# A float32 gradient matmul on one core: four warm-up matmuls in place of 55, and a new order of visits on every engine

## The chip, the cores and the metric

The kernel runs on one core of one Trainium2 chip. The metric is device time in microseconds (us) of one execution, lower is better; the figure is the median of several runs. A core has five engines with queues of their own: TensorE (PE in the profile; its weight loads are PEld), VectorE (DVE), ScalarE (ACT), GpSimd (POOL) and SyncE (SP), and 16 DMA engines that move data between the chip's memory and the on-chip memory.

## The reference

```python
batch, m, k, n = 16, 512, 1024, 768
# input: batch x m x k, grad_output: batch x m x n, both float32
grad_weight = np.einsum('bmk,bmn->kn', input, grad_output)   # 1024 x 768, float32
```

With batch and m taken together this is one product: X transposed times G, where X has 8192 rows of 1024 and G 8192 rows of 768. The sum runs over the 8192 rows.

## The kernel before

**Units.** The 8192 rows come in 32 units of 256 rows, two groups of 128 (128 is the height of TensorE's array). The loads convert to bf16 on the way and are issued by GpSimd, for each unit first `gp` (rows of G), then `xp` (rows of X), L170 to L182. The first 128 rows of unit 0, and the X rows behind them, come in float32 (`gf`, `xf`) by the queues of SyncE and ScalarE and are cast in pieces on VectorE and ScalarE (`round_by`, L222 to L240; the tokens r0 to r4 below are five of these pieces). Ten buffers hold units (`PAIRS_HELD`).

**Blocks.** The 1024 x 768 result is cut into four blocks: A and B are the upper 512 rows, left and right 384 columns, C and D the lower rows, left and right. Each block has four tiles of 128 x 384, numbered 0 to 3 (`q`). Units 0 to 4 and 31 (kind "s" in `LOADS`) are multiplied plainly: each of their two row groups adds one matmul to each of the 16 tiles. The 26 units between (kind "P") are multiplied with seven products in place of eight, by sums of halves made on VectorE: `sum_x` (three instructions, L206, L208, L210) and `sum_g` (L216, L218, L220) into `xe` and `ge`, and two of them back into the unit's own buffers. The seven products are the streams A, B, C and 1, 5, 6, 7; A and 1 share one accumulation. At the end the streams 1, 5, 6, 7 are combined into A to D by VectorE and GpSimd (`close` with `final`, `merge`).

**Banks and sums.** TensorE adds up in eight banks of its accumulator memory. Stream A stays in banks 0, 1 and 2 all the time, packed (`PLACES`): tiles 1 and 2 are split in a 256- and a 128-column piece, so that a matmul of A1 or A2 is two instructions. All other tiles share the remaining banks: a tile gets a few matmuls, then its sum is moved out and the bank goes to another tile. There are four ways to move sums:

- `close` (L348): the bank is copied or added to the tile's sum in on-chip memory (`acc`, `macc`), on VectorE (token v, an addition, L371) or on ScalarE (token c, a copy, only where nothing has to be added, L367);
- `fill` (f, L302): ScalarE copies the tile's sum into a bank first, so that TensorE goes on adding to it;
- `set_aside` (z, L383): the bank is copied into one of 24 spare tiles, `aside`, and
- `add_aside` (y, L392) adds it to the sum later, on VectorE.

**Order.** All of it is written out by hand: `PLAN` is a list of tokens, and the loop at L401 emits them one after the other; nothing is reordered afterwards. Each engine runs its own instructions in the order of the list. A token such as `C1@6.1` is one matmul of tile C1 into bank 6, opened there; `A2.1` is one more matmul of A2; `vC1`, `cC3` close a tile; `fD1@6` fills bank 6 with D1; `zcC2.0` sets C2 aside by ScalarE into spare tile 0, `yC2.0` adds it; `g0.5` is the first of the three sums of G's part of unit 5, `x2.5` the last of X's; `wC1` is a merge on GpSimd. Finished tiles are stored by SyncE's queue (one piece by ScalarE's), the first of them in two halves.

**Warm-up.** Ahead of the first product TensorE multiplies constants (L156 to L164) while the first data are on their way: one matmul of 512 columns, then 54 of 80 columns with a stationary operand of 32 columns, all bf16, each with a weight load of its own.

```python
WARMUP = [("b", 512)] + [("s", 80)] * 54
```

Of the kernel before, what the change touches and what calls it, by code (L numbers as in the profile page):

```python
# [9 lines left out]
P = 128  # L10
# [1 line left out]
LOADS = "sssssPPPPPPPPPPPPPPPPPPPPPPPPPPs"  # L12

PLAN = (
    "A2.1 C1@6.1 C3@3.1 C2@4.1 vC1 C0@5.1 cC3 A0.1 A1.1 r0 cC2 A3.1 B2@7.1 D0@3.1 r1 r3 D2@6.1 D1@4.1 r2 "
    "r4 vB2 C0.1 cD0 A0.1 vD1 A1.1 B1@7.2 cD2 B3@3.2 vB1 B0@6.2 cB3 D3@4.2 vB0 C3@7.1 C2@3.1 cD3 A2.1 vC3 "
    "A3.2 fD1@6 A1.1 vC2 D0@7.2 fB2@4 D1.2 fD2@3 vD0 B2.2 cD1 C0.1 D2.2 vB2 C1@7.2 cD2 B0@6.2 vC1 B1@4.2 "
    "B3@3.2 vB0 C2@7.2 vB1 fC3@6 A0.2 vB3 A2.2 D3@4.2 vC2 C3.2 vD3 B2@3.1 C1@7.1 cC3 C0.1 vB2 A1.1 D0@4.1 "
    "D1@6.1 vC1 A3.1 D2@3.1 vD0 fB0@7 vD1 C0.2 B1@4.2 vD2 B2@6.2 vB1 B0.2 B3@3.2 vB2 cB0 C2@4.2 vB3 A0.2 "
    "zcC2.0 D2@6.2 fD3@3 C3@7.2 yC2.0 D0@4.2 zcD2.1 vC3 D3.2 D1@6.2 vD0 cD3 C1@7.2 yD2.1 A3.4 fB3@3 vD1 "  # L30
    "A2.4 vC1 D3@4.2 A1.4 zcD3.0 B1@6.2 yD3.0 B3.2 vB1 C2@4.2 cB3 D0@7.2 vC2 D2@6.2 zcD0.1 C3@3.2 vD2 "
    "fD1@4 C0.2 B0@7.2 zvC3.0 C1@6.2 yD0.1 zcB0.2 B2@3.4 vC1 D1.4 yC3.0 vB2 D0@7.2 cD1 C3@6.2 yB0.2 "
    "zcD0.1 A0.2 g0.5 A0.2 fC2@4 D3@7.2 zvC3.0 C2.2 g1.5 zcD3.2 B1@6.2 yD0.1 cC2 D2@3.2 zvB1.3 B3@7.2 "
    "zcD2.1 B0@4.1 g2.5 B0.1 zcB3.4 C1@6.1 x0.5 C1.2 zcB0.5 A2.3 yC3.0 zcC1.6 10@3.1 x1.5 12@7.1 A1.3 c10 "
    "yD3.2 c12 C2@4.1 x2.5 C3@6.1 C0.1 zcC2.0 g0.6 C0.2 zcC3.2 11@3.1 yB1.3 13@7.1 A3.2 c11 g1.6 A3.1 c13 "
    "50@4.1 yD2.1 51@6.1 52@3.1 c50 A0.1 g2.6 53@7.1 x0.6 c51 A0.1 70@4.1 C0.1 c52 A1.1 v53 71@6.2 c70 "
    "72@3.1 x1.6 72.1 c71 73@7.2 yB3.4 c72 60@4.2 x2.6 61@6.2 c73 g0.7 62@3.2 c60 63@7.2 v61 c62 A2.1 "
    "g1.7 B0@4.2 c63 yC1.6 B2@3.2 zcB0.3 B1@6.1 g2.7 B1.1 A3.1 zcB2.1 yB0.5 13@4.2 zcB1.4 11@7.1 x0.7 "
    "11.1 A2.1 zc13.6 A0.1 v11 C0.1 C1@3.2 x1.7 10@6.2 zcC1.5 yC2.0 B3@4.2 zc10.7 53@7.1 g0.8 53.1 A3.1 "
    "A1.1 zc53.0 x2.7 70@3.2 vB3 51@6.2 zc70.8 C2@7.1 g1.8 C2.1 zc51.9 yC3.2 12@4.2 C3@3.1 zcC2.10 g2.8 "  # L40
    "C3.1 A1.1 x0.8 A0.1 zcC3.2 50@7.2 52@6.3 v12 zc50.11 71@3.1 x1.8 71.1 zc52.12 A2.1 yB0.3 72@4.2 "
    "zc71.13 73@7.1 g0.9 73.1 zc72.3 A3.1 x2.8 61@6.2 zc73.14 g1.9 63@3.2 v61 C0.1 60@4.2 zc63.15 g2.9 "
    "B2@7.2 y13.6 zc60.16 B1@6.2 zcB2.17 10@3.1 x0.9 10.1 A3.1 f62@4 C0.1 vB1 A2.1 zc10.6 50@7.2 x1.9 "
    "62.2 zc50.18 yB2.1 C2@3.2 c62 51@6.1 x2.9 51.1 A1.1 fB0@7 g0.10 A0.1 B3@4.3 vC2 B0.2 zcB3.1 g1.10 "
    "B0.1 12@3.2 v51 cB0 11@4.1 g2.10 11.1 zc12.19 13@6.3 yB1.4 zc11.20 C3@7.1 x0.10 C3.2 C1@3.3 v13 "
    "53@4.1 x1.10 53.2 zcC1.4 70@6.3 vC3 zc53.21 x2.10 52@3.2 zc70.22 g0.11 71@7.2 zc52.23 61@4.2 yC1.5 "
    "A2.1 f62@6 A0.1 g1.11 B2@3.2 v71 62.2 zcB2.5 C0.1 g2.11 A1.1 c62 x0.11 A1.1 A3.2 f73@3 72@7.2 v61 "
    "f60@6 A2.1 73.1 x1.11 73.2 f12@4 v72 60.3 c73 x2.11 12.2 c60 g0.12 63@7.3 c12 y53.0 B1@3.3 f10@6 "
    "g1.12 11@4.2 v63 10.2 zc11.0 g2.12 A0.1 C2@7.3 vB1 c10 C0.1 x0.12 f51@4 C0.1 B0@6.2 f50@3 51.3 vC2 "
    "x1.12 50.3 f52@7 vB0 A0.1 c51 52.1 g0.13 52.1 c50 A1.1 13@4.1 x2.12 13.1 fB3@6 A2.1 g1.13 C1@3.2 c52 "  # L50
    "v13 B3.3 fC3@7 g2.13 A3.1 vC1 53@4.2 cB3 C3.1 x0.13 C3.2 f70@3 C0.1 A0.1 f71@6 v53 70.3 cC3 x1.13 "
    "71.3 c70 y10.7 72@4.2 c71 x2.13 72.1 61@7.1 g0.14 f62@3 61.2 A1.1 v72 fB2@6 A2.1 62.2 g1.14 f10@4 "
    "62.1 v61 B2.3 c62 g2.14 10.2 f11@7 x0.14 10.1 A3.2 cB2 12@3.3 v10 f73@6 x1.14 11.3 v12 73.2 c11 "
    "x2.14 73.1 60@4.1 f63@3 g0.15 60.2 C0.1 c73 y70.8 A0.1 63.2 fB0@7 g1.15 63.1 B1@6.3 v60 c63 B0.1 "
    "g2.15 fC1@4 B0.2 vB1 A1.2 fC2@3 x0.15 A2.2 f13@6 C1.3 vB0 C2.2 cC1 x1.15 C2.1 13.3 y51.9 f50@7 C0.1 "
    "g0.16 cC2 51@4.3 c13 x2.15 50.2 g1.16 f52@3 50.1 v51 53@6.3 c50 g2.16 52.3 fC3@4 v53 A0.2 fB3@7 "
    "x0.16 C3.3 c52 yC2.10 B3.3 f72@6 x1.16 cC3 70@3.3 vB3 72.2 f62@4 g0.17 72.1 f71@7 A3.2 x2.16 62.2 "
    "c72 g1.17 62.1 71.3 v70 fB2@6 C0.1 c62 g2.17 B2.3 v71 f11@4 61@3.1 x0.17 61.2 f12@7 11.3 cB2 v61 "
    "12.2 c11 x1.17 12.1 73@6.3 yC3.2 c12 10@3.1 x2.17 10.2 f60@7 g0.18 63@4.3 v73 60.3 g1.18 fB1@6 A1.2 "
    "v10 A2.2 c60 g2.18 B1.3 v63 A0.2 x0.18 cB1 C0.2 f50@4 C1@3.3 y52.12 A3.1 x1.18 A3.1 50.3 vC1 B0@7.1 "  # L60
    "x2.18 B0.2 c50 g0.19 13@6.3 fC2@3 vB0 A1.1 f53@4 A2.1 C2.1 g1.19 C2.2 v13 53.3 cC2 g2.19 51@7.1 "
    "x0.19 f52@6 51.2 A0.1 c53 A2.1 v51 52.3 f70@3 x1.19 52.1 fC3@4 61@7.3 y50.11 c52 C3.1 g0.20 C3.2 "
    "f72@6 70.1 x2.19 70.2 cC3 g1.20 72.3 v61 c70 C0.1 g2.20 B3@4.4 c72 y71.13 fB2@7 A1.2 y72.3 f71@6 "
    "A3.2 x0.20 B2.3 vB3 12@3.3 cB2 x1.20 71.4 v12 62@7.1 g0.21 62.3 c71 x2.20 f63@3 60@4.2 g1.21 60.1 "
    "f10@6 A0.1 v62 63.3 g2.21 f11@7 10.4 v60 c63 x0.21 11.4 fC1@4 v10 fB1@3 C0.2 c11 A2.1 x1.21 A2.1 "
    "C1.3 y63.15 f73@6 fB0@7 B1.1 x2.21 B1.2 g0.22 cC1 73.4 cB1 y60.16 B0.1 f13@4 g1.22 B0.3 v73 C2@3.2 "
    "cB0 g2.22 C2.1 13.1 x0.22 f51@6 13.3 f53@7 vC2 A1.2 c13 51.1 x1.22 51.3 f50@3 y73.14 53.2 c51 x2.22 "
    "53.2 g0.23 50.4 c53 yB2.17 A0.2 f52@7 g1.23 A3.2 c50 y10.6 70@6.2 g2.23 70.1 f72@3 C3@4.4 y50.18 "
    "x0.23 A2.2 C0.2 v70 72.3 x1.23 f61@6 72.1 52.3 vC3 c72 x2.23 52.1 61.2 g0.24 c52 61.2 y12.19 B3@4.3 "
    "c61 g1.24 B3.1 f12@7 B2@3.4 y11.20 f62@6 g2.24 12.1 x0.24 12.3 62.3 vB2 c12 A1.2 vB3 c62 60@7.2 "  # L70
    "x1.24 f71@3 60.1 A0.1 g0.25 A0.1 fB1@4 A3.2 x2.24 f63@6 71.2 g1.25 71.2 v60 B1.2 c71 g2.25 B1.2 "
    "yB3.1 63.3 f11@3 x0.25 63.1 cB1 C1@7.4 c63 y53.21 11.2 f10@4 x1.25 11.2 f73@6 vC1 10.3 c11 x2.25 "
    "10.1 fC2@7 73.1 g0.26 73.3 c10 yC1.4 C2.2 fB0@3 g1.26 C2.2 c73 y70.22 13@4.3 cC2 g2.26 B0.4 y52.23 "
    "f50@6 x0.26 f53@7 A2.3 cB0 50.4 v13 f51@3 x1.26 53.4 f70@4 v50 51.1 g0.27 51.3 f61@6 x2.26 c53 70.2 "
    "g1.27 70.2 c51 yB2.5 B3@7.2 c70 g2.27 B3.1 61.3 y11.0 f52@3 C0.1 fC3@4 x0.27 C0.3 c61 A1.3 vB3 x1.27 "
    "A0.3 fB2@7 x2.27 C3.2 g0.28 C3.2 52.2 cC3 g1.28 52.2 72@6.1 g2.28 72.3 c52 A3.3 v72 B2.2 x0.28 f62@6 "
    "B2.2 12@4.2 cB2 x1.28 12.2 60@3.1 f71@7 x2.28 60.4 v12 62.1 g0.29 62.4 fB1@4 v60 B1.2 c62 g1.29 B1.2 "
    "f11@3 g2.29 71.4 vB1 63@6.2 c71 x0.29 63.2 11.4 v63 A2.1 x1.29 fC1@6 A2.2 v11 C2@4.3 g0.30 f13@3 "
    "C2.1 10@7.1 x2.29 10.3 vC2 C1.2 g1.30 C1.2 f11@4 v10 13.3 cC1 g2.30 13.1 A1.1 x0.30 A1.2 c13 12@6.2 "
    "f13@3 11.1 x1.30 10@7.1 A0.3 c11 v12 13.1 x2.30 f61@4 C0.3 v10 f62@6 61.4 v13 f60@7 62.2 f63@3 v61 "  # L80
    "60.2 A3.3 v62 f71@4 63.2 v60 f72@6 71.2 v63 f70@7 A0.2 A1.2 v71 f73@3 A2.3 f51@4 wC1 A3.2 73.5 vA3 "
    "vA0 72.3 v73 51.4 vA1 f53@3 wC3 70.4 vA2 53.4 v72 f52@0 v70 fC1@1 C0.2 52.3 v51 fC2@2 f50@6 C1.3 wB1 "
    "fC3@7 vC0 C2.3 fD1@4 v52 C3.5 cC1 wB2 fD2@5 50.4 v53 fB1@1 fD3@0 D2.2 wB3 B1.4 vC2 cC3 fB2@3 v50 "
    "D1.2 cB1 D3.2 B2.5 fD0@2 vD2 fB0@7 vD3 D0.2 fB3@1+6 vB2 B0.7 vD0 vD1 B3.6 vB0 cB3 "
).split()


WARMUP = [("b", 512)] + [("s", 80)] * 54
PAIRS_HELD = 10
SUMS_HELD = 8  # L90
ASIDE = 24

MERGED = 2


PACKED = True
PLACES = {
    0: [(0, 0, 0, 384)],
    1: [(0, 384, 0, 128), (1, 0, 128, 384)],
    2: [(1, 256, 0, 256), (2, 0, 256, 384)],  # L100
    3: [(2, 128, 0, 384)],
}

HALVED = 3


@with_exitstack
def kernel(  # L110
    ctx: ExitStack,
    tc: tile.TileContext,
    input: bass.AP,
    grad_output: bass.AP,
    out: bass.AP,
):
    nc = tc.nc
    bf16 = mybir.dt.bfloat16
    f32 = mybir.dt.float32
# [34 lines left out]

    wps = psum.tile([P, 512], f32, name="bank7")
    for dt, cols in WARMUP:  # L156
        rows = 32 if dt == "s" else P
        nc.tensor.matmul(
            wps[0:rows, 0:cols],
            nc.const_aps.tensor(1.0, (P, rows), bf16),  # L160
            nc.const_aps.tensor(1.0, (P, cols), bf16),
            start=True,
            stop=True,
        )  # L164
# [4 lines left out]
    for u, kind in enumerate(LOADS):  # L169
# [15 lines left out]
        tiles[u] = (xp, gp)  # L185
        if kind == "P":
            items.append(("P", u, None))

    extra = {}
# [77 lines left out]
            return macc[:, SLOT[p], q, :]  # L270
        row = q if p in "AB" else Q + q
        return acc[:, row, LEFT if p in "AC" else RIGHT]

    SHARED = {"A": "1", "B": "6", "C": "7", "D": "5", "6": "1", "7": "6"}
# [180 lines left out]
```

## Time and profile before

| | |
|---|---|
| time, median of 3 runs | 161.84 us (161.83 to 162.16) |
| profiled execution, first to last instruction (span) | 160.0 us |
| the median over that span | 1.84 us |
| PE busy, matmuls | 155.1 us, 1057 |
| DVE busy, instructions | 146.8 us, 344 |
| ACT busy, instructions | 118.2 us, 274 |
| POOL busy | 39.6 us |
| loaded and stored by the core's DMA engines | 33.42 MB, mean 209 GB/s |
| matmul of 384 columns, start to start, full clock | 0.162 us |
| first real matmul, last real matmul (starts) | 5.29 us, 156.43 us |

The profile is of one execution, and its own time is the span of 160.0 us with what lies around the first and last instruction, which the median puts at 1.84 us. The busy time of an instruction is its latency: VectorE and ScalarE begin the next one before the last has ended, so that an addition of 128 x 384 that is listed with 0.55 us follows another after 0.46 us. Matmuls overlap in the same way: 0.326 us listed, 0.162 us from start to start.

| line, engine | what | number, mean |
|---|---|---|
| L328 PE | matmul, 128 x 384 | 838, 0.33 us |
| L371 DVE | add a bank to a sum | 83, 0.56 us |
| L392 DVE | add a spare tile to a sum | 46, 0.56 us |
| L206 to L220 DVE | sums of halves, six for each of 26 units | 156, 0.36 to 0.69 us |
| L302 ACT | fill a bank from a sum | 118, 0.48 us |
| L367 ACT | close a bank by copying | 107, 0.48 us |
| L383 ACT | set a bank aside | 43, 0.48 us |

### The profile page before, as it was taken

The numbers are of one execution on the slowest core, as the hardware profiler recorded it, in microseconds if no ns is written. First come the engines' busy times: TensorE is split into PE (matmuls) and PEld (weight loads), VectorE is DVE, ScalarE is ACT, GpSimd is POOL, SyncE is SP. The second block draws the span as 40 slices with busy tenths as digits, with TensorE's granted clock in tenths as the row PEclk, the third lists the DMA queues.
The fourth block names the chain that finished last, engine by engine and source line by source line (L and its number), as shares of the span: only waits on it lengthen the run. The fifth ranks groups of instructions, "written<-read, shape, count | busy, mean of one in ns | idle before, by whom it ended". The sixth has DMA issues, their size and how long they took to land.

```text
span 160.0 us, 3074 instructions
## 1 busy us (share of the span) xinstructions
PE 155.1 (97%) x1057; PEld 98.4 (62%) x1057; DVE 146.8 (92%) x344; ACT 118.2 (74%) x274; POOL 39.6 (25%) x74
## 2 busy tenths in 40 slices
PE   8999899999999999999999999999999999999991
PEld 7666476666666666666656666666666666656661
DVE  0689979999999999999999999999999989998991
ACT  3683444899788788988986596985789855685960
POOL 7442222122221222222122221222222100004510
PEclk9999999999999999999999999999999999999999
DMA  5999999999999999999999999999999999931786
GB/s 174 298 211 215 212 216 213 211 215 212 212 213 213 212 211 213 213 214 214 216 215 213 212 211 214 212 213 210 212 217 212 212 215 215 212 64 45 218 294 234
DMA packets 12447, 33.42 MB, mean 209 GB/s; under 512 B 1424, under 2 KB 4240, under 8 KB 12432
## 3 DMA queue, kind: packets, MB, share of 16 engines
q0 software_dynamic: 9360, 28.64, 90.5%
q1 hardware_dynamic: 2640, 3.41, 6.6%
q10 hardware_dynamic: 432, 1.18, 2.0%
q8 instruction: 8, 0.13, 0.3%
q14 instruction: 7, 0.06, 0.1%
HBM read 58.72 MB, written 3.15 MB: 387 GB/s over the span
## 4 chain that ended last, share of the span: by engine, by line
PE 85%; DMA 8%; POOL 2%; ACT 1%; issue 1%; DVE 1%; ACTq 0%; POOLq 0%
PE bank L328 85%; DMA xp<-in_input_dram 8%; POOL gp L180 1%; POOL xp L182 1%; ACT bank L302 1%; ACT acc L367 1%; DVE acc L369 1%; POOL gp L175 0%; ACT macc L367 0%; ACTq L367 0%; POOLq L441 0%
## 5 line engine op out<-in xcount | busy, mean ns | idle before, releaser
L328 PE MATMUL bank<-gp,xp 128*128 128x384 bf16 (+2 forms) x690 | 109.1, 308 | 0.8 <-DMA xp<-in_input_dram 0.5
L328 PEld LDWEIGHTS <-xp 128*128 128x128 bf16 x690 | 64.6, 98 | 37.9 <-DMA xp<-in_input_dram 0.8
L328 PE MATMUL bank<-ge,xe 128*128 128x384 bf16 x312 | 59.7, 326 | 0.0
L328 PEld LDWEIGHTS <-xe 128*128 128x128 bf16 x312 | 30.3, 98 | 19.0
L302 ACT COPY bank<-macc 128x384 f32<-128x384 f32 x73 | 34.4, 486 | 7.0 <-DVE macc L371 2.5
L367 ACT COPY macc<-bank 128x384 f32<-128x384 f32 x68 | 31.4, 482 | 5.7 <-PE bank L328 5.0
L176 POOL DMA_DIRECT2D xp<-in_input_dram x30 | 15.9, 529 | 53.0 <-DVE ge L218 21.0
L367 ACT COPY acc<-bank 128x384 f32<-128x384 f32 (+1 forms) x39 | 18.3, 477 | 12.3 <-PE bank L328 12.2
L175 POOL DMA_DIRECT2D gp<-in_grad_output_dram x30 | 15.9, 531 | 37.4 <-DMA gp<-in_grad_output_dram 10.4
L371 DVE TENSOR_TENSOR acc<-bank,acc 128x384 f32<-128x384 f32 x45 | 23.7, 555 | 0.6 <-PE bank L328 0.4
L302 ACT COPY bank<-acc 128x384 f32<-128x384 f32 (+2 forms) x45 | 20.9, 480 | 4.3 <-DVE acc L371 1.9
L383 ACT COPY aside<-bank 128x384 f32<-128x384 f32 x43 | 19.1, 483 | 6.0 <-PE bank L328 5.1
L371 DVE TENSOR_TENSOR macc<-bank,macc 128x384 f32<-128x384 f32 x38 | 21.2, 558 | 0.6 <-PE bank L328 0.5
L206 DVE TENSOR_TENSOR xe<-xp 128x1024 bf16<-128x1024 bf16 x26 | 18.0, 692 | 0.0
L392 DVE TENSOR_TENSOR acc<-acc,aside 128x384 f32<-128x384 f32 x26 | 14.5, 556 | 1.3 <-ACT aside L383 1.3
L216 DVE TENSOR_TENSOR ge<-gp 128x768 bf16<-128x768 bf16 x26 | 14.5, 558 | 0.0
L392 DVE TENSOR_TENSOR macc<-macc,aside 128x384 f32<-128x384 f32 x20 | 11.2, 563 | 0.0
L210 DVE TENSOR_TENSOR xp<-xp,xe 128x512 bf16<-128x512 bf16 x26 | 11.0, 425 | 0.1
L208 DVE TENSOR_TENSOR xe<-xe,xp 128x512 bf16<-128x512 bf16 x26 | 11.0, 424 | 0.1
L399 POOL TENSOR_TENSOR acc<-acc,macc 128x384 f32<-128x384 f32 x5 | 5.0, 1000 | 21.6 <-DVE macc L364 19.7
L220 DVE TENSOR_TENSOR gp<-ge,gp 128x384 bf16<-128x384 bf16 x26 | 9.3, 358 | 0.1
L218 DVE TENSOR_TENSOR ge<-gp,ge 128x384 bf16<-128x384 bf16 x26 | 9.3, 359 | 0.0
(20 smaller groups left out, 42.7 us busy)
## 6 DMA issues: line engine op xcount, KB each, us to landing
xp<-in_input_dram POOLq DMA_DIRECT2D x30, 512.0 KB, 16.9
gp<-in_grad_output_dram POOLq DMA_DIRECT2D x30, 384.0 KB, 16.8
out_dram<-acc SPq DMA_DIRECT2D x12, 192.0 KB, 2.0
xf<-in_input_dram ACTq DMA_DIRECT2D x2, 512.0 KB, 5.0
gp<-in_grad_output_dram POOLq DMA_DIRECT2D x3, 192.0 KB, 6.4
out_dram<-acc SPq DMA_DIRECT2D x6, 96.0 KB, 2.2
xp<-in_input_dram POOLq DMA_DIRECT2D x2, 256.0 KB, 7.8
gf<-in_grad_output_dram SPq DMA_DIRECT2D x2, 192.0 KB, 4.4
```

Source lines behind the costliest of these rows:

```text
L175: nc.gpsimd.dma_start(out=gp, in_=G[rows, :].rearrange("(p m) n -> p m n", m=2))
L176: nc.gpsimd.dma_start(out=xp, in_=X[rows, :].rearrange("(p m) k -> p m k", m=2))
L206: nc.vector.tensor_sub(out=xe[:, 0:2, :], in0=x[:, 1::-1, :], in1=x[:, 3::-2, :])
L208: nc.vector.tensor_sub(out=xe[:, 2, :], in0=xe[:, 0, :], in1=x[:, 0, :])
L210: nc.vector.tensor_add(out=x[:, 1, :], in0=x[:, 2, :], in1=xe[:, 2, :])
L216: nc.vector.tensor_add(out=ge[:, 0:2, :], in0=g[:, 0:2, :], in1=g[:, 1::2, :])
L302: nc.scalar.copy(out=tile_[:, t0 : t0 + c1 - c0], in_=sum_of(p, q)[:, c0:c1])
L328: nc.tensor.matmul(tile_[:, t0 : t0 + c1 - c0], stat, mov[:, c0:c1], start=start, stop=True, skip_group_check=True,)
L367: nc.scalar.copy(out=d, in_=b)
L371: nc.vector.tensor_add(out=d, in0=b, in1=d)
L383: copy(out=aside[i], in_=b[:, t0 : t0 + NH])
L392: nc.vector.tensor_add(out=dst, in0=dst, in1=aside[i])
```

## The change

The warm-up becomes four matmuls of 512 columns: bf16, float32, float32, bf16, each with a stationary operand of 128 columns. `PLAN` is replaced as a whole; the order of the loads, the buffers, the sums and all helpers stay. What is in the two lists:

| | before | after |
|---|---|---|
| TensorE instructions (matmuls and weight loads) | 2114 | 2008 |
| real matmuls, columns | 1002, 353,280 | 1001, 353,280 |
| bank added to a sum by VectorE (L371) | 83 | 114 |
| bank copied to a sum by VectorE (L369) | 20 | 10 |
| set aside (z) and added later (y) | 46 | 14 |
| fills (f) | 117 | 87 |
| closed by ScalarE (c) | 107 | 85 |
| merges on GpSimd (w) | 5 | 3 |

The sums of a unit (g and x tokens) stand more or less evenly spread between matmuls before, and often several in a row after. The diff, with the middle of both lists left out:

```diff
 PLAN = (
-    "A2.1 C1@6.1 C3@3.1 C2@4.1 vC1 C0@5.1 cC3 A0.1 A1.1 r0 cC2 A3.1 B2@7.1 D0@3.1 r1 r3 D2@6.1 D1@4.1 r2 "
-    "r4 vB2 C0.1 cD0 A0.1 vD1 A1.1 B1@7.2 cD2 B3@3.2 vB1 B0@6.2 cB3 D3@4.2 vB0 C3@7.1 C2@3.1 cD3 A2.1 vC3 "
...
-    "60.2 A3.3 v62 f71@4 63.2 v60 f72@6 71.2 v63 f70@7 A0.2 A1.2 v71 f73@3 A2.3 f51@4 wC1 A3.2 73.5 vA3 "
-    "vA0 72.3 v73 51.4 vA1 f53@3 wC3 70.4 vA2 53.4 v72 f52@0 v70 fC1@1 C0.2 52.3 v51 fC2@2 f50@6 C1.3 wB1 "
-    "fC3@7 vC0 C2.3 fD1@4 v52 C3.5 cC1 wB2 fD2@5 50.4 v53 fB1@1 fD3@0 D2.2 wB3 B1.4 vC2 cC3 fB2@3 v50 "
-    "D1.2 cB1 D3.2 B2.5 fD0@2 vD2 fB0@7 vD3 D0.2 fB3@1+6 vB2 B0.7 vD0 vD1 B3.6 vB0 cB3 "
+    "r0 r2 A0.1 A1.1 C1@7.1 A2.1 C0@5.1 A3.1 D2@4.1 B0@6.1 B3@3.1 vB3 r1 cC1 cD2 r3 cB0 D0@7.1 B1@4.2 A1.1 "
+    "C3@3.2 D3@6.2 vB1 vC3 vD3 cD0 r4 D1@7.2 B2@4.2 A0.1 C2@3.3 D0@6.1 D1.1 A2.1 A0.1 vB2 vC2 cD1 B3@4.2 A2.1 "
...
+    "A1.1 60.3 63.2 73.5 A2.2 A1.2 A0.2 v71 v60 v63 g2.30 x2.30 vA2 vA1 v73 f70@4 f72@6 wC1 70.4 72.3 A3.3 "
+    "C0.3 v70 v72 vA0 vC0 vA3 fC1@7 fD1@1 fC3@3 f52@4 f51@6 f53@5 fD3@0 wC2 D1.2 52.3 C3.4 51.4 53.4 C1.3 v52 "
+    "v51 vC3 vD1 fB1@4 fD2@2 fC2@6 f50@3 B1.5 D3.2 D2.2 C2.4 50.4 vB1 v53 vD2 vD3 v50 fD0@4 cC1 fB2@5 fB0@7 "
+    "cC2 wB3 D0.2 B2.5 B0.8 vB2 vD0 vB0 fB3@3+0 B3.5 cB3 "
 ).split()

-WARMUP = [("b", 512)] + [("s", 80)] * 54
+WARMUP = [("b", 512), ("f", 512), ("f", 512), ("b", 512)]
...
     for dt, cols in WARMUP:
-        rows = 32 if dt == "s" else P
+        kind = f32 if dt == "f" else bf16
         nc.tensor.matmul(
-            wps[0:rows, 0:cols],
-            nc.const_aps.tensor(1.0, (P, rows), bf16),
-            nc.const_aps.tensor(1.0, (P, cols), bf16),
+            wps[:, 0:cols],
+            nc.const_aps.tensor(1.0, (P, P), kind),
+            nc.const_aps.tensor(1.0, (P, cols), kind),
             start=True,
             stop=True,
         )
```

## The prediction

> **What bounds the kernel now.** I read the page first, then who TensorE waited for, the chain that ended last in order of time, the timeline around TensorE's one wait, and the DMA records just before it.
>
> ```profile
> span 160.0 us, 3074 instructions
> PE 155.1 (97%) x1057; PEld 98.4 (62%) x1057; DVE 146.8 (92%) x344; ACT 118.2 (74%) x274; POOL 39.6 (25%) x74
> DMA  5999999999999999999999999999999999931786
> ```
> TensorE (PE) is busy from end to end; the loads fill the DMA engines up to about 143 us. TensorE's waits, whole list:
> ```profile
> PE bank L158 <- PEq L441: 0.8, 1, 0.8
> PE bank L328 <- DMA xp<-in_input_dram: 0.5, 1, 0.5
> PE bank L328 <- ACT xp L224: 0.2, 1, 0.2
> ```
> Only one wait lies inside the work. In the chain it is the seam between a landing and one unbroken run of matmuls:
> ```profile
> 4.53 12.36 DMA xp<-in_input_dram
> 16.89 0.05 issue
> 16.93 62.51 PE bank L328 x417
> ...
> 82.28 74.04 PE bank L328 x490
> ```
> And in the timeline (start, length, idle before in brackets):
> ```profile
> 15.82 0.65 PE L328 MATMUL bank<-gp,xp 128*128 128x384 bf16 x3
> 15.87 1.94 DVE L371 TENSOR_TENSOR acc<-bank,acc 128x384 f32<-128x384 f32 x4
> ...
> 16.93 0.66 PE L328 MATMUL bank<-gp,xp 128*128 128x384 bf16 x3 [0.46 <-DMA xp<-in_input_dram]
> ```
> The 0.46 counts from the modelled end of a pipelined matmul. By starts: the one before began at 16.14 and a 384-column matmul takes 0.162 start to start, so TensorE was ready at 16.30 and lost 0.63. The only other hole is at 82.28: 0.42 between two starts, 0.25 lost, behind a chain of ScalarE and VectorE copies. So the time is: ready at 16.30, data at 16.93, then 139.3 us of matmuls, 0.25 lost, last matmul begun at 156.43, and 3.57 us of closing, last store and landing up to 160.0.
>
> Why was that data late? It is unit 2's `xp`. Its 16 DMA engines report from 15.59 to 16.89: fifteen by 16.16, one 0.73 later. The load before it came in within 0.55 (13.14 to 13.69). In between stands one packet of another kind, 5.4% of 16 engines over 1.1 us, so 0.95 us of one engine:
> ```profile
> q0 software_dynamic: 59, 0.24, 107.5%
> q8 instruction: 1, 0.02, 5.4%
> ```
> It is 16 KB of instructions; eight come in the span, at 13.3, 34.6, 51.1, 71.1 and so on, when TensorE has started 215, 504, 722, 986 instructions (weight loads counted): about every 256. The engine that carried the first stays late: unit 3's `xp` has fifteen engines by 20.51 and the last at 21.20.
>
> TensorE's clock is half speed at the start, though the printed column says 1.00 in both rows (the first clock record is at 6.40):
> ```profile
> 5.28:6.40 1.12, 1.11 (x5) 0.69 (x6) 1.00 1.08 298
> 6.40:7.52 1.12, 1.12 (x10) 0.71 (x8) 1.00 1.17 209
> ```
> Five matmuls against ten; a 384-column one takes 0.320 before 6.40 and 0.162 after.
>
> **The change, part by part.** All in this execution's time; the median of the runs (161.84) stands 1.84 above its span, and I carry that over.
>
> *Warm-up length.* Before: 512 columns in 0.515 start to start, then 54 of 80 columns at 0.067, from 0.78 to 5.07, where the first cast pieces (4.83 to 5.24) let the work begin at 5.29. Now two bf16 of 512 columns (0.515 each) and two fp32 ones, for which the trace has no row. Bounds from the 0.515 row: an fp32 operand has twice the bytes of a bf16 one, so one to four bf16 products each: 0.5 to 2.1 us. The warm-up ends between 2.8 and 5.9. I take four at the columns' pace (4 x 0.427 = 1.71, the rest hidden behind the next weights): end 5.05, nothing gained or lost; the upper end costs 0.65 at the start. [...]
>
> *Fewer instructions.* 110 TensorE instructions of warm-up become 6. The 215th instruction, at which the first fetch came, is now about real matmul 102 instead of 51. That is at 5.21 + 14.67 (102 matmuls at 0.162, 0.109 and 0.056) + 0.60 (cold) + 0.24 (below) = 20.7. Unit 2's `xp` then lands with the fifteen, at 16.16, and unit 3's at about 20.5. [...]
>
> *The order up to unit 2.* Both orders put 72 real matmuls with the same 24,576 columns ahead of the first read of unit 2's `xp`: 10.42 us at full clock. The new one begins with block A, which needs VectorE's first cast (4.83, 0.33) and not ScalarE's: start 5.21 against 5.29. Cold time adds half of 5.21 to 6.40, 0.60. A new wait: bank 4 (D2) is closed by ScalarE and opened again by B1 three matmuls later. Matmul to its signal 0.34, ScalarE copy 0.48, two hops 0.07 make 0.89; D2 and the three matmuls cover 0.65; wait 0.24. Arrival 5.21 + 10.42 + 0.60 + 0.24 = 16.47, behind the landing at 16.16: no wait, 0.46 earlier than 16.93.
>
> *Unit 3.* Read 31 matmuls later (4.40 us): 20.87, data at 20.5. Slack 0.36.
>
> *The rest.* Behind the read of unit 2 both orders have 328,704 columns: 139.28 us. 16.47 + 139.28 = 155.75. VectorE has 12 operations fewer (46 set-aside sums become 14, additions from a bank 83 become 114), ScalarE 81 fewer copies, some 39 us; both counted at nothing, because TensorE's list shows no wait for either after the first cast. What replaces them near the end: with seven fills in a row, VectorE frees a bank each 0.46 (four additions in 1.94 above: (1.94 - 0.55)/3), while the block in front (D1.2) covers 0.33; then ScalarE's fill comes a hop late. I count 0.2 there and 0.2 for the same pattern at the fill of B2 in bank 5. The hole like that at 82.28 may or may not have a successor: half, 0.13. Small waits at fills in between: 0 to 0.2, taken 0.1. Stores, SP's queue and the load order are unchanged in number and order, and the last block is again a 128-column piece of B3 closed by VectorE: 3.57 again.
>
> Sum: 155.75 + 0.4 + 0.13 + 0.1 = 156.38 against 156.43, so 161.79; without the last two and with holes of 0.1 it is 155.95, so 161.36. The wait at 0.24 is surer than those behind it, so I take a value between, nearer the full sum: 161.7. About 0.32 us (0.2%) is what a measurement of this kernel can tell from no change.
>
> **Rivals.**
>
> A, more is gained: the fill waits do not show and no hole follows at mid-run. 155.75 + 0.1 + 3.57: 161.26 to 161.5. For it: ScalarE has 39 us less to do. Against: 0.46 per closing is VectorE's, not ScalarE's.
>
> B, the landing does not move, or the fetch catches unit 3 instead. Then 16.93 stays (161.79 + 0.46 = 162.25), or 21.24 takes the place of 20.87 (161.79 + 0.37 = 162.16). It decides if the fetch comes before about 20.1. For it: the margin between 20.1 and 20.7 is four matmuls. Against: the load under way at 13.3 was not delayed, only the next.
>
> C, less slack. A set-aside frees a bank without waiting for VectorE's queue; with 14 instead of 46, VectorE's bunched sums wait for a landing with the closings queued behind them, and TensorE waits for those banks. Any landing more than some 0.2 to 0.4 late (unit 3: 0.36) then costs the excess in full. The second fetch, at 34.6, made one load 0.6 late (last engine at 36.73); it now falls near 42. Price 0.2 to 0.6: 162.0 to 162.4.
>
> D, the slower side: the warm-up no longer warms. If four long matmuls end early or do not count as activity, the clock rises later than 6.4. Each microsecond later costs half, as nothing absorbs it now that the landing is early; from 6.5 on the sum exceeds the old time, from 7.1 on by 0.2%. If it must start counting at the first real matmul, 5.6 us (0.78 to 6.40) behind 5.21 is 10.8: (10.8 - 6.4)/2 = 2.2, up to 161.79 + 2.2 = 164.0. Against: by columns the new warm-up is as long as the old.
>
> **How the numbers follow.** The sum above has 0.45: 161.4 to 161.95, a third of it faster by over 0.2%. A 0.10, all faster. B 0.17, a third of it within. C 0.16, a third of it within. D 0.12, slower. Together faster 0.25, within 0.42, slower 0.33. The range 161.25 to 162.7 leaves out most of D, and edges of A and C.
>
> **What would show it.** Right: no wait at 16.9; the first instruction packet near 20.7; unit 2's `xp` landed by 16.2 and unit 3's by 20.6; matmuls at 0.162 from about 6.4; waits of 0.2 near 7.7, 147 and 153. Wrong: a wait of `bank` for `xp` at 16.9 or 21.2 (B), many waits of TensorE for VectorE or ScalarE from 25 us on (C), 0.320 matmuls after 7 us (D).

## The result, and the profile after

The changed kernel took 162.63 us (median of 10 runs, 162.15 to 163.23) against 161.97 for the kernel before (10 runs, 161.83 to 162.27): ratio 1.0043, interval 1.0028 to 1.0058. It became slower by 0.66 us where 161.7 was forecast.

The page of the changed kernel, its first lines and the DMA row of the 40 slices:

```profile
span 160.8 us, 2836 instructions
PE 155.6 (97%) x1007; PEld 96.0 (60%) x1007; DVE 143.1 (89%) x332; ACT 85.2 (53%) x193; POOL 37.8 (24%) x72
DMA  4999999999999999999999999999999999913785
```
TensorE is as full as before, ScalarE has 33 us less to do, and the span is 0.8 longer. So the time is at an end of the run, or in holes too small to move a share. TensorE's waits, whole list:

```profile
PE bank L136 <- PEq L416: 0.8, 1, 0.8
PE bank L303 <- DVE gp L200: 0.3, 1, 0.3
```
The wait for `xp` is gone, and the chain of waits shows one unbroken run of 989 matmuls from 8.00 on, where the one before had its seams at 16.93 and 82.28:

```profile
6.70 0.37 DVE gp L200
7.07 0.04 issue
7.11 0.34 PE bank L303
7.45 0.02 issue
7.47 0.49 ACT acc L342
7.96 0.04 issue
8.00 148.76 PE bank L303 x989
```
The last matmul began at 156.53, before it was 156.43. From there to the end of the span, the tail from here on, it took 3.55 before and 4.30 now (the spans are 159.97 and 160.82 in the trace). In that stretch only the last closing and the stores are left. The stores, by the tile they write (minimum, median and maximum duration of an issue in ns, then the time from issue to landing); first before, then after:

```profile
L346 SPq DMA_DIRECT2D out_dram<-acc x19: 332/388/602, 145.9 to 157.1; - x19
DMA to landing us min/median/max: 1.9/2.1/2.2
```
```profile
L321 SPq DMA_DIRECT2D out_dram<-acc x19: 333/402/1053, 145.6 to 157.2; - x19
DMA to landing us min/median/max: 1.9/2.7/3.9
```
One issue of a store held SP for 1.053 us, and a store landed up to 3.9 us after its issue. The DMA queues of that moment (152.8 to 154.4) show what else was there:

```profile
q1 hardware_dynamic: 329, 0.46, 79.4%
q8 instruction: 1, 0.02, 5.5%
```
A packet of 16 KB of instructions, the eighth of the run, came at 152.86, in the midst of the stores' data (q1), and took 1.40 us on one of the 16 DMA engines (5.5% of 16 engines over 1.6 us). Before, the eighth came at 144.20, between the last load (landed 142.7) and the data of the first store (from 147.0 on). The window from 143.5 to 145.7 of the kernel before holds nothing else:

```profile
DMA packets 1, 0.02 MB, mean 7 GB/s; under 512 B 0, under 2 KB 0, under 8 KB 0
...
q8 instruction: 1, 0.02, 3.9%
```
What the packet did to the stores, from the records of their landings (a store counts as landed when all 16 DMA engines have reported):

| store issued (after) | 15 engines by | the 16th | lag |
|---|---|---|---|
| 151.23 | 153.07 | 153.11 | 0.04 |
| 151.69 | 153.62 | 155.57 | 1.94 |
| 152.18 | 154.14 | 156.05 | 1.92 |
| 153.10 | 154.95 | 156.53 | 1.58 |
| 153.57 (held SP until 154.63) | 156.16 | 156.99 | 0.83 |
| 155.19 | 157.24 | 157.93 | 0.69 |
| 156.18 | 158.32 | 158.91 | 0.59 |
| 157.20, the last | 159.44 | 159.93 | 0.48 |

Before, the 16th was at most 0.04 behind the 15th in these last stores, and the last one, issued at 157.10, landed at 159.07. The 0.86 in its landing is 0.10 of issue, 0.31 of the fifteen engines (2.25 after the issue in place of 1.94; why is not shown) and 0.45 of the one that was behind (0.48 in place of 0.03). The records name no engine: that the late one is the one that took the packet is inferred from the times.

### The profile page after: what moved, and what is told of

Its sections match the earlier page's. It is cut to its first block, busy times and chain, and to the rows that moved or that the text cites. A ratio compares the mean times of both kernels' runs of the same rounds, so it can differ in the third digit from the quotient of the medians.

```text
span 160.8 us, 2836 instructions
## 1 busy us (share of the span) xinstructions
PE 155.6 (97%) x1007; PEld 96.0 (60%) x1007; DVE 143.1 (89%) x332; ACT 85.2 (53%) x193; POOL 37.8 (24%) x72
## 4 chain that ended last, share of the span: by engine, by line
PE 93%; DMA 3%; DVE 0%; ACT 0%; SPq 0%; issue 0%; DVEq 0%
PE bank L303 93%; DMA gf<-in_grad_output_dram 3%; ACT acc L342 0%; SPq L128 0%; DVE gp L200 0%; DVE acc L344 0%; DVEq L344 0%
## 5 line engine op out<-in xcount | busy, mean ns | idle before, releaser
L303 PE MATMUL bank<-ge,xe 128*128 128x384 bf16 x312 | 61.6, 326 | 0.0
L277 ACT COPY bank<-macc 128x384 f32<-128x384 f32 x57 | 27.0, 485 | 21.5 <-DVE macc L346 11.7
L346 DVE TENSOR_TENSOR acc<-bank,acc 128x384 f32<-128x384 f32 x62 | 32.6, 552 | 5.2 <-PE bank L303 4.9
L342 ACT COPY macc<-bank 128x384 f32<-128x384 f32 x58 | 26.9, 480 | 17.7 <-PE bank L303 17.2
L346 DVE TENSOR_TENSOR macc<-bank,macc 128x384 f32<-128x384 f32 x52 | 28.2, 552 | 0.9 <-PE bank L303 0.6
L277 ACT COPY bank<-acc 128x384 f32<-128x384 f32 (+2 forms) x31 | 14.4, 473 | 15.0 <-DVE acc L346 11.7
L342 ACT COPY acc<-bank 128x384 f32<-128x384 f32 (+1 forms) x27 | 12.7, 477 | 8.5 <-PE bank L303 8.3
L358 ACT COPY aside<-bank 128x384 f32<-128x384 f32 x14 | 6.6, 480 | 5.6 <-PE bank L303 5.5
L374 POOL TENSOR_TENSOR acc<-acc,macc 128x384 f32<-128x384 f32 x3 | 3.0, 1001 | 24.5 <-DVE macc L339 20.3
L339 DVE TENSOR_TENSOR acc<-bank,macc 128x384 f32<-128x384 f32 (+2 forms) x15 | 6.7, 497 | 0.3 <-PE bank L303 0.2
```

What stands on the lines that cost most here:

```text
L277: nc.scalar.copy(out=tile_[:, t0 : t0 + c1 - c0], in_=sum_of(p, q)[:, c0:c1])
L303: nc.tensor.matmul(tile_[:, t0 : t0 + c1 - c0], stat, mov[:, c0:c1], start=start, stop=True, skip_group_check=True,)
L342: nc.scalar.copy(out=d, in_=b)
L346: nc.vector.tensor_add(out=d, in0=b, in1=d)
```

## Experiments

The first four ran beside 29 runs of the kernel before (161.89, 161.72 to 162.13), the other four on another chip beside 23 (161.94, 161.74 to 162.31). The tool of most of them is to change how many instructions TensorE gets, and so where each packet falls, without changing its columns: 384-column matmuls that continue a sum are cut in pieces of 256 and 128, a matmul and a weight load more for each. Later diffs show only the lines that differ from this one.

```diff
+SPLIT_FROM, SPLITS = 800, 54
...
+                cuts = [(c0, c1)]
+                count[0] += 1
+                if count[0] >= SPLIT_FROM and count[1] < SPLITS and not start and c1 - c0 == 384:
+                    count[1] += 1
+                    cuts = [(c0, c0 + 256), (c0 + 256, c1)]
+                for a0, a1 in cuts:
+                    nc.tensor.matmul(
...
```

**The changed kernel with 54 late cuts** (the diff above, on the changed kernel):

> The changed kernel, with 54 of its 384-column matmuls behind the 800th cut into a 256- and a 128-column one (same banks, same sums): 108 more TensorE instructions in the stretch around 125 to 140 us, so that the eighth instruction packet comes some 8 us earlier, near 144 to 145, behind the last load and ahead of the first store. Theory 1 (that packet, at 152.9 among the stores of the changed kernel, holds one DMA engine for 1.4 us and delays the last landing by 0.76): its cost goes, 54 cuts cost 54 x 0.0025 to 0.005 = 0.14 to 0.27, so 162.63 - 0.76 + 0.2 = 162.1 (161.9 to 162.2); last store landed within 2.0 us of its issue. Theory 2 (the new order's last stores stand too close together, whatever the packet does): no gain, 162.8. Theory 3 (the loss lies in the new order's waits at 7 and 8 us): no gain, 162.8.

Measured: 161.64 (11 runs, 161.43 to 161.97), ratio 0.9991 (0.9983 to 1.0) to the kernel before. With 108 instructions more, the kernel lost all of its deficit, 0.3 more than the lower end of what was expected. Its page and its stores:

```profile
span 159.8 us, 2944 instructions
...
out_dram<-acc SPq DMA_DIRECT2D x12, 192.0 KB, 2.0
```
The eighth packet came at 144.13 and took 0.93. No issue from 150 us on took longer than 0.42, the 16th engine was 0.03 behind in the last store, and the last matmul at 156.29 was followed by 3.48 to the end.

**The old order with the new warm-up** (against the kernel before; the warm-up's loop as in the changed one):

```diff
-WARMUP = [("b", 512)] + [("s", 80)] * 54
+WARMUP = [("b", 512), ("f", 512), ("f", 512), ("b", 512)]
...
```

> The order of before with the four-matmul warm-up alone. Theory 1: the first instruction packet moves from 13.3 to near 21 and unit 2's xp lands at 16.2 to 16.3, but the eighth moves from 144.2 to about 152 to 153, among the stores: the wait at 16.9 shrinks by up to 0.6, of which VectorE's old order may give back most, and the tail grows by 0.5 to 0.9: 161.97 - 0.3 + 0.76 = 162.4 (162.0 to 162.8). Theory 2 (the loss is the new order's): no tail, 161.97 - 0.6 to 161.97, so 161.4 to 162.0.

Measured: 162.51 (6 runs, 162.07 to 162.68), ratio 1.0035 (1.0022 to 1.0048). The loss is there without the new order:

```profile
L333 SPq DMA_DIRECT2D out_dram<-acc x19: 333/411/1574, 145.6 to 157.7; - x19
```
The packet came at 152.72 and took 1.54; the tail is 4.73. The stuck issue was worse here (1.574): the last store went out at 157.68, 1.52 behind the start of the last matmul (156.16), where the changed kernel and the one before have 0.67. By then the late engine had caught up (the 16th 0.03 behind in the last store, landed at 159.98). The same packet is paid by SP's queue instead of by one engine's lag. The early landing of unit 2's `xp` (16.22) was worth less than its 0.63: TensorE then waited 0.27 and 0.14 at the same place for VectorE.

**The new order with the old warm-up** (against the changed kernel):

```diff
-WARMUP = [("b", 512), ("f", 512), ("f", 512), ("b", 512)]
+WARMUP = [("b", 512)] + [("s", 80)] * 54
...
```

> The new order with the old warm-up of 55. Theory 1: the packets are where they were before (13.3 and about 144), so no tail, but unit 2's xp lands at 16.9 again: TensorE waits there for 0.45 on the sum that I made (16.47 to 16.93), and unit 3's xp at 21.2: 161.97 + 0.3 to 0.5 = 162.3 to 162.5. Theory 2 (the new order's stores): 162.6 and more, with the last store landing over 2.4 us behind its issue.

Measured: 162.04 (11 runs, 161.93 to 162.49), ratio 1.0011 (1.0002 to 1.0019): some 0.3 better than expected. With the long warm-up the packets are where they were before (the first at 13.37, the eighth at 144.52) and the tail is 3.48. The wait for unit 2 is back, 0.49 by starts at 16.99; its `xp` was complete at 16.95:

```profile
PE bank L316 <- DMA xp<-in_input_dram: 0.3, 1, 0.3
PE bank L316 <- DVE gp L212: 0.3, 1, 0.3
```
So the late landing of unit 2 does go with the first packet, as the prediction had it (complete at 16.95 with the packet at 13.37, at 16.31 with it at 20.95); and the new order without the new warm-up is no gain either: the last matmul began at 156.76.

**The old order, the new warm-up and 54 late cuts** (against the kernel before):

```diff
-WARMUP = [("b", 512)] + [("s", 80)] * 54
+WARMUP = [("b", 512), ("f", 512), ("f", 512), ("b", 512)]
...
+SPLIT_FROM, SPLITS = 800, 54
...
```

> The order of before, the four-matmul warm-up, and 54 late matmuls cut in two as in the first run: the first packet near 21 and the eighth near 144. Theory 1: early gain without the tail: 161.97 - 0.0 to 0.6 + 0.2 = 161.6 to 162.2, and 0.5 to 0.8 below the same order without the cuts. Theory 2: 0.2 above the same order without the cuts.

Measured: 161.57 (11 runs, 161.51 to 161.75), ratio 0.9983 (0.9975 to 0.9992): faster than the kernel before and than the changed one, and 0.94 below the same order without the cuts, where 0.5 to 0.8 was expected.

```profile
L342 SPq DMA_DIRECT2D out_dram<-acc x19: 332/391/605, 145.7 to 156.9; - x19
DMA to landing us min/median/max: 1.9/2.1/2.2
```
Packet eight at 143.91, last matmul at 156.22 (0.21 earlier than before), tail 3.55. The early landing is worth 0.2 to 0.3 when the last packet is kept out of the stores. With both packets placed alike, the new order (161.64) is not better than the old (161.57).

**The changed kernel once more**, on the second chip:

> The changed kernel again, beside the three runs of this group. Theory 1 (the eighth instruction packet near 153 holds one DMA engine among the stores): 162.4 to 162.8, with fifteen engines done with the last store about 0.5 to 0.7 ahead of the sixteenth. Theory 2 (stores too close together): the same time, but the engines spread evenly.

Measured: 162.77 (6 runs, 161.95 to 162.94), ratio 1.0053 (1.004 to 1.0066). The run that was profiled is the 161.95, the quickest of all its runs, and it shows the same thing in a milder form: the packet at 153.13 took 0.93, one issue was stuck for 1.201, the 16th engine was 1.60 behind at most and 0.01 in the last store, where the theory expected 0.5 to 0.7; tail 4.00. Nor did the engines spread evenly, as the other theory had it. The 0.45 that this tail is longer than before is 0.12 in the issue of the last store (0.79 behind the start of the last matmul, 0.67 before) and 0.34 in its landing (2.28 after the issue in place of 1.94, for all sixteen engines).

**The kernel before with 75 late cuts**, so that a ninth packet comes:

```diff
+SPLIT_FROM, SPLITS = 800, 75
...
```

> The kernel before, with 75 of its 384-column matmuls behind the 800th cut in a 256- and a 128-column one: 150 TensorE instructions more, so that a ninth instruction packet comes, near 152 to 153, among its stores. Nothing else is changed: the old order, the old warm-up. Theory 1: 75 x 0.0025 = 0.2 for the cuts and 0.6 to 0.9 for the packet: 161.89 + 0.8 to 1.1 = 162.7 to 163.0. Theory 2 (the loss belongs to the new order or the new warm-up): 161.89 + 0.2 = 162.1.

Measured: 163.41 (6 runs, 162.93 to 163.97), ratio 1.0091 (1.0075 to 1.0107). This gives the old warm-up and the old order the fault of the changed kernel, and shows too that cutting matmuls gains nothing by itself. The stores, and the DMA window from 154.4 to 156.2:

```profile
L355 SPq DMA_DIRECT2D out_dram<-acc x19: 332/451/1902, 146.5 to 159.1; - x19
...
DMA to landing us min/median/max: 1.9/2.2/4.1
```
```profile
q1 hardware_dynamic: 250, 0.33, 52.1%
q8 instruction: 1, 0.02, 5.6%
```
The ninth packet came at 154.45 and took 1.63. SP was stuck in an issue from 154.55 to 156.45, and the last store went out at 159.07, 2.00 behind the start of the last matmul (0.67 in the kernel before); tail 5.11. It lost more than expected, most of it through SP. (Its profiled run, at 163.97 the slowest, also waited until 17.39 for unit 2's `xp`, 0.46 longer than the profile of before. Whether the other five runs had this wait is not shown; the tail alone is 1.56 longer, about the 1.47 that the median lost.)

**The changed kernel with 20 late cuts**, which move the packet by some 2 us:

```diff
+SPLIT_FROM, SPLITS = 800, 20
...
```

> The changed kernel with 20 cuts in place of 54: the eighth packet comes some 3 us earlier than in the changed kernel, near 150, among the first stores and not the last. Theory 1: the delayed engine has six stores more to catch up in, so less than half of the 0.7 to 0.9 is left: 162.0 to 162.4, between the changed kernel and the one with 54 cuts. Theory 2 (any number of cuts helps for another reason, such as the spacing of matmuls): a gain in proportion, 20/54 of it, so 162.2 to 162.3, but with no lag of one engine at the last store that is smaller than in the changed kernel.

Measured: 161.93 (11 runs, 161.48 to 162.32), ratio 0.9999 (0.9989 to 1.001), a little better than expected. The packet came at 150.73, also among the stores' data, and took 1.05; but the lag of the 16th engine was 0.61 in a store that landed at 154.20, 0.23 at 155.62 and 0.03 in the last, and no issue was stuck:

```profile
L330 SPq DMA_DIRECT2D out_dram<-acc x19: 332/406/602, 146.0 to 157.6; - x19
```
So a packet among the stores is not enough to lose time; it also matters when it comes. Its length is not what decides: in the changed kernel's second profile a shorter packet (0.93) stuck an issue for 1.201 and left a tail of 4.00. Two things differ in the moment, and this run does not separate them. The packet came 8.8 us before the last landing (7.1 and 6.1 in the two profiles of the changed kernel), so the late engine had more time to catch up; and the order issues no store between 150.82 and 151.62, most of the packet's time, so none was there to be stuck.

This profile also has a wait that the others of the new order lack: TensorE lost 0.36 at 61.16 on an `xp` whose 16th engine was 0.56 behind, just after the third packet (59.10). So the new order has little slack for a packet among the loads too, as rival C feared.

**The changed kernel with 54 cuts early** (from the 130th matmul on), so that the cuts lie far from the end:

```diff
+SPLIT_FROM, SPLITS = 130, 54
...
```

> The changed kernel with the 54 cuts behind the 130th matmul instead of the 800th: the eighth packet again near 144, and the second to seventh 8 us earlier too. Theory 1: only the instructions ahead of the eighth packet count, not where the cuts are: as with the late cuts, 161.6 to 161.9, if the tight order finds no landing late; up to 0.4 more where the second packet, then near 31 to 32, delays a load beyond the order's slack. Theory 2 (late cuts relax something near the end): 162.5 to 162.9.

Measured: 161.75 (11 runs, 161.44 to 161.93), ratio 0.9986 (0.9978 to 0.9995). Last packet at 144.29, tail 3.48. For the time of the last packet only the count of instructions mattered here, not where they were added (144.29 with the cuts early, 144.13 with them late); that rules out the cuts' own effect on the closings and stores near the end.

All ten profiles side by side, last packet and tail:

| kernel | last packet, us long | stuck issue of a store | tail |
|---|---|---|---|
| before | 144.20, 1.39 | none | 3.55 |
| after | 152.86, 1.40 | 1.053, to 154.63 | 4.30 |
| new order, 54 late cuts | 144.13, 0.93 | none | 3.48 |
| old order, new warm-up | 152.72, 1.54 | 1.574, to 154.63 | 4.73 |
| new order, old warm-up | 144.52, 1.03 | none | 3.48 |
| old order, new warm-up, 54 cuts | 143.91, 0.99 | none | 3.55 |
| after, once more | 153.13, 0.93 | 1.201, to 154.43 | 4.00 |
| before, 75 cuts | 154.45, 1.63 | 1.902, to 156.45 | 5.11 |
| new order, 20 cuts | 150.73, 1.05 | none | 3.47 |
| new order, 54 early cuts | 144.29, 1.02 | none | 3.48 |

In all four with a packet at 152.7 or later, an issue was stuck, and it came free 0.36 to 0.37 us after the packet's end (152.86 + 1.40 = 154.26, and 154.63; the others alike). The other six have tails of 3.47 to 3.55.

## Why the prediction was wrong, by its own steps

**The step that failed** is the last of "The rest": "Stores, SP's queue and the load order are unchanged in number and order, and the last block is again a 128-column piece of B3 closed by VectorE: 3.57 again." It was 4.30. (3.57 takes the span as 160.0; with the trace's 159.97 it is 3.55.) That is 0.75 of the 0.85 between the two profiled spans, and about as much as the median lost (0.66). The prediction counted 104 instructions fewer of warm-up and followed the first packet (13.3 to 20.7), mentioned the second, and stopped there. (The trace has 98 fewer: each fp32 matmul shows as two matmuls and two weight loads, so the new warm-up is 12 records and not 6, and TensorE's records are 2014 in all, not 2008.) The same subtraction applies to the eighth: it came when TensorE had started 1955 instructions before and 1969 after, but 110 of the former and 12 of the latter are warm-up, so it moved by some hundred instructions of products, 8.7 us, into the stores. The count, the packet's time and the times of the stores were all in the trace of before.

**The first packet and unit 2** came as forecast: packet at 20.95 (20.7), unit 2's `xp` complete at 16.31 (16.16), unit 3's at 20.66 (20.5), no wait for either. Rival B did not happen. The eight packets of the changed kernel came 256, 259, 257, 256, 269, 239 and 214 started instructions of TensorE apart. These runs show 0.75 us of tail for one packet (4.30 against 3.55) and a wait of half a microsecond for another (0.49 at 16.99, new order with the old warm-up).

**The warm-up** came as taken:

```profile
L136 PE MATMUL bank<-const-float32-1.0 128*128 128x512 f32 x4 | 3.6, 1057 | 0.0
L136 PE MATMUL bank<-const-bfloat16-1.0 128*128 128x512 bf16 x2 | 1.2, 607 | 0.8 <-PEq L416 0.8
```
The two fp32 matmuls show as four records, 0.853 apart from start to start, so 1.71 each, the figure that the prediction took as its own choice within its bounds of 0.5 and 2.1; no row of the kernel before shows it. The first real matmul began at 5.22 (5.21). The first clock record is at 6.22 (6.40 before), and a 384-column matmul took 0.320 from start to start at 5.83 and 0.163 at 6.36, so rival D did not happen:

```profile
5.22:6.22 1.00, 1.00 (x5) 0.68 (x6) 1.00 1.07 342
6.24:7.24 1.00, 0.74 (x6) 0.40 (x5) 1.00 1.18 228
```
Five matmuls in the first row; the second has six although TensorE stood still for 0.42 of it.

**That 0.42** was not forecast. Two rows of the timeline from 6 to 8.3 us:

```profile
6.70 0.36 DVE L200 CAST gp<-gf 128x384 bf16<-128x384 f32 x1 [1.20 <-DMA gf<-in_grad_output_dram]
7.11 1.37 PE L303 MATMUL bank<-gp,xp 128*128 128x384 bf16 x6 [0.26 <-DVE gp L200]
```
D2 needs the right half of the first G rows, whose last DMA engine reported at 6.67 (the others by 6.02), in the profile of before at 6.15. It is not one late landing, though: in all six profiles of the new order the same matmul lost 0.34 to 0.61 behind the same cast, 0.34 also where the piece had landed at 6.12. In the four profiles of the old order the matmul behind this cast lost 0 to 0.13. So it is the new order that reads this piece too early, and it gives back here much of the 0.63 that it saves at unit 2; the slack before `xp` of unit 2 (16.47 against 16.16) was counted without it.

**The bank of D2:** the wait forecast as 0.24 was 0.24, at 8.00. **The small waits** were counted at 0.63 (0.4 at the late fills, 0.13 at mid-run, 0.1 between) and measured at 0.46 (seven above 0.03, the largest 0.14). The two late fills that were put at 0.2 each cost 0.09 (147.59) and 0.05 (153.65), and nothing above 0.03 was left at mid-run.

So TensorE's sum is 156.38 + 0.42 (right half of G) + 0.01 (start) - 0.10 (0.50 of cold time in place of 0.60) - 0.17 (small waits) = 156.54, and 156.53 was measured. That the prediction's 156.38 came so near is in part luck: 0.43 was left out of it and 0.27 counted too much. VectorE and ScalarE were rightly counted at nothing: rival C would show many waits from 25 us on, and the largest is 0.14.

**Rival A** was right that the small waits are small, but it kept the old tail like the sum, and its 161.26 to 161.5 was farther off than 161.7. None of the four rivals had a packet in the stores.

## What to carry to other kernels

With 98 records fewer on TensorE's queues every one of the eight instruction packets moved, by 5.2 to 9.1 us (the first from 13.33 to 20.95, the eighth from 144.20 to 152.86), not the next one alone; the other engines were not tried. So list all the packets of the trace, shift each by the instructions added or removed, and look at what the DMA engines do at the new times, to the last store. A packet between the last load and the first store, where the DMA engines were idle here, cost the tail nothing (3.48 to 3.55 with one at 143.91 to 144.52, 4.00 to 5.11 with one at 152.72 or later); a few instructions added can buy that place, as the old order with the new warm-up and 54 cuts shows (161.57, against 162.51 without the cuts). And a gain of half a microsecond at the start says little before the last microseconds, where 0.75 us were lost here, have been gone through as closely.

## What the runs showed of the hardware that was not expected

- A 16 KB packet of instructions held one DMA engine for 0.9 to 1.6 us, and an issue of a store on SP's queue that fell beside it stuck for 1.053 to 1.902: in all four profiles with a packet at 152.7 or later it came free 0.36 to 0.37 us after the packet's end. What held the issue is not shown.
- The lag of one engine shrank over the stores that followed (1.94 to 0.48 in one profile of the changed kernel, 1.60 to 0.01 in the other), so how much of it was paid depended on what was left to store. That is probably why the changed kernel spreads more (162.15 to 163.23) than the one before (161.83 to 162.27). Between these two profiles the packet's length (1.40 or 0.93) and its moment (152.86 or 153.13) both differ, so what makes the spread stays open.
- The first clock record came between 3.84 and 6.40 us in the ten profiles: 6.40, 5.54 and 4.78 with the long list of warm-up matmuls, 3.84 to 6.22 with the four. Nothing in the kernels explains the spread, and the end of a run does not follow it.
